# A transformer block's down projection: where a chain of weight sums is read and summed, and the order of its last joins

## The chip, the cores and the metric

The kernel runs on one core of a Trainium2 chip. A core has a matrix engine (TensorE, PE in the profile, with its weight loads shown as PEld), a vector engine (VectorE, DVE), a scalar engine (ScalarE, ACT), a general engine (GpSimd, POOL), a queue engine that mostly issues DMAs (SyncE, SP), and 16 DMA engines between the memory (HBM) and the on-chip memory (SBUF). Matmul results stand in PSUM, eight banks of 128 x 512 float32 here.

The metric is the device time of one execution in microseconds (us). Times of a kernel are given as the median of several runs; the profile is of one further execution.

## The reference

The reference is one block: a mixer (a convolution branch and a state-space branch, gated), and then a gated feed forward, each with norms and a residual. The change lies in the end of the feed forward:

```python
h = rms_norm(x, ffn_pre_g[i])
gt, up = jnp.split(h @ w_gate_up[i], 2, axis=-1)
f = (jax.nn.silu(gt) * up) @ w_down[i]
x = x + rms_norm(f, ffn_post_g[i])
```

There are 512 tokens of 1024 features; the feed forward is 2816 wide, so `w_down` has 22 strips of 128 rows, and all numbers are float32.

## The kernel before

**Products in three parts.** For float32 accuracy every operand is split in two: `hi` is a cast on ACT to the matrix engine's input type, `lo` is the remainder, which DVE computes as source minus `hi`. A product is then three matmuls (`mm3`, lines 170 to 172): hi by hi, hi by lo, lo by hi. A weight piece ("form") is therefore a read of 128 x 1024 numbers (512 KB) into a raw tile (5 buffers, tag `raw`), a cast on ACT and a subtraction on DVE.

**Feed forward.** The loop over `u` (22 units, of 84 matmuls of 256 columns) makes the gate and up projections; `second(u)` and `third(u)` are parts of a unit, and the last `third` runs after the loop. Its pieces are read by SP, in the order in which the program names them (`w_raw`, `keep_in_program_order`).

**Down projection.** The first 16 strips of `w_down` are multiplied by a scheme of seven products (p1, p5, p6, p3, p7, p2, p4 in this order) on two-by-two blocks: tokens, strips and output features each cut in halves; the blocks of the weights are s11, s12, s21, s22, each of four pieces j = 0 to 3 (512 KB each). So there are 28 jobs (p, j), each of 12 matmuls of 512 columns (2 halves of the piece by 2 token blocks by 3). The remaining six strips ("d") are multiplied directly: 8 matmul groups of 3 for each, for four token blocks t and two output halves n. Some products need sums of weight blocks:

- p1 needs s11, p5 needs s11+s12, p6 needs s11+s12+s22, p4 needs s11+s12+s22+s21. These come from a **chain**: a tile `chain[j]` is read with s11, and after each use the next block is added to it by an accumulating DMA which POOL issues (`chain_add`, line 1063).
- p3 needs s22 and p2 needs s21, read into raw tiles by SP (`raw_read`, line 1058). p7 needs s12+s22: SP reads s12 and POOL adds s22 by an accumulating DMA (line 1060).

p1 takes pieces j = 0, 1 from raw tiles (their reads and casts come before the feed forward's end, lines 1111 to 1113) and j = 2, 3 from the chain. All four chain tiles lie in the pool `pf`, which takes the room of the feed forward's operands and opens when `third` of the last unit is done (`h2.close()`, line 1115). There SP reads the chain in the order 2, 3, 0, 1 (line 1121), and s12 is added to j = 0 and 1 at once; for j = 2 and 3 the addition follows p1's form.

**Order.** Each engine runs its instructions in a fixed order. Except where the program holds an order (`keep_in_program_order` for SP's reads), a planner chooses that order at build time from the dependencies, the program order and its own estimate of durations. `prepare(n)` names the forms up to `S_AHEAD` = 4 jobs ahead and the raw reads up to `R_AHEAD` = 7 jobs ahead; a form's tiles come from nine pairs (5 `whi`, 4 `phi`). The banks x, v, y take the products as `PRODUCTS` (line 1033) lists them: p1, p6, p7 and p4 go to x, p5 and p3 to v, p2 to y; the bank z holds strips of the direct part alone. After p1, p5 and p6 ACT copies the banks into tiles `ev` (line 1158), so that they can be used again; in the trace such a tile is `evp`, a bank `sx`, `sv`, `sy`, `sz`.

**The end.** For each token block t, and first for the half n = 1, then n = 0, three last strips are multiplied; the bank is joined with its `ev` tile on DVE (line 1200). Then `scale_of` (line 1201) squares both halves on ACT (`mean_sq`, line 778), and `factor` turns the two sums into a scale `rs` (a small addition on DVE, a power on POOL, line 786). DVE multiplies both halves by the gain (line 1203), and `store(t - 1)` scales the block before, adds the residual `x2` (read from `x2d`) and sends it out (lines 1184 and 1187).

Of the kernel before, what the change touches and what calls it, by code (L numbers as in the profile page):

```python
# [10 lines left out]
F32 = mybir.dt.float32  # L11
# [3 lines left out]
ALU = mybir.AluOpType  # L15
# [3 lines left out]
P = 128  # L19
# [13 lines left out]
NF = FF // P  # L33
# [43 lines left out]
DMA_FROM = 8  # L77

NPAIR = 8
NQ = NPAIR // 2  # L80
S_AHEAD = 4
R_AHEAD = 7
# [19 lines left out]
ORDER += [("gu", _i) for _i in range(2 * EARLY_U, 2 * NF)]  # L102
ORDER += [("wd", _i) for _i in range(2 * NPAIR, NF)]
W_END = len(ORDER)
ORDER += [(_b, _j) for _b in BLOCKS for _j in range(NQ)]

# [7 lines left out]
def block_kernel(ctx: ExitStack, tc: tile.TileContext, x, xT, prm, hp, gp, w, out):  # L114
    nc = tc.nc
    act, dve, pe, pool = nc.scalar, nc.vector, nc.tensor, nc.gpsimd
# [11 lines left out]
    seq = {key: n for n, key in enumerate(ORDER)}  # L128
# [58 lines left out]
    def col(name, i):  # L187
        o = PRM_OFF[name] + i
        return prm_t[:, o : o + 1]
# [17 lines left out]
    def va_tile(name):  # L207
        return sp.tile([P, T], F32, tag="va", bufs=VA_BUFS, name=name)
# [58 lines left out]
    for k in range(NK):  # L267
# [3 lines left out]
        if k % 4 == 0:  # L271
# [3 lines left out]
            out=elo[k], in0=xk[k], scalar=col("pre_g", k), in1=ehi[k].bitcast(F32), op0=ALU.mult, op1=ALU.subtract,  # L275
# [3 lines left out]
    for k in range(NK):  # L279
# [3 lines left out]
        else:  # L283
            sq = va_tile(f"sq{k}")
# [148 lines left out]
    for j in range(NK):  # L433
# [11 lines left out]
        if j == 0:  # L445
            for k in range(NK):
                for ps, n in ((pv, "val"), (pg, "glu")):
                    wh, wl = w_get(n, 0)
                    c = slice(k * P, (k + 1) * P)
# [325 lines left out]
    def mean_sq(src, pool_, tag, n):  # L775
        ss = sm.tile([P, 1], F32, tag=f"ss{n}", bufs=2, name=f"ss{n}_{tag}")
        jk = pool_.tile([P, T], BF16, tag="jk", bufs=1, name=f"jk{n}_{tag}")
        mark["sq"] = act.activation(jk, src, AF.Square, scale=D**-0.5, accum_out=ss)
        return ss

    def factor(ss, tag):

        rs = sm.tile([P, 1], F32, tag="rs1", bufs=2, name=f"rs_{tag}")
        m = sm.tile([P, 1], F32, tag="pm1", bufs=2, name=f"pm_{tag}")
        dve.tensor_scalar(out=m, in0=ss[0], scalar1=ss[1], scalar2=RMS_EPS, op0=ALU.add, op1=ALU.add)
        pool.tensor_tensor(out=rs, in0=m, in1=neg_half[:, :1], op=ALU.pow)
        return rs

    def scale_of(srcs, pool_, tag):
        return factor([mean_sq(srcs[n], pool_, tag, n) for n in range(2)], tag)  # L790

    cols2 = [slice(0, T), slice(T, D)]
# [26 lines left out]
    def g_raw(u, i):  # L819
        n = seq[("gu", 2 * u + i)]  # L820
        for r in range(n, min(n + RAW_AHEAD, seq[("wd", 2 * NPAIR)])):
            w_raw(r)
        return raws[n]
# [17 lines left out]
    def prep_s(u):  # L841

        if u >= NF or (u, "s1") in forms:
            return
        ra, rb_ = g_raw(u, 0), g_raw(u, 1)
        (a11, a12), (a21, a22) = [(r[:, :T], r[:, T:]) for r in (ra, rb_)]
        s1_ = w2.tile([P, T], F32, tag="s1", bufs=2, name=f"s1_{u}")
        dve.tensor_tensor(out=s1_, in0=a21, in1=a22, op=ALU.add)
        dve.tensor_tensor(out=a21, in0=a11, in1=a21, op=ALU.add)
        dve.tensor_tensor(out=a11, in0=s1_, in1=a11, op=ALU.add)  # L850
        dve.tensor_tensor(out=a12, in0=a11, in1=a12, op=ALU.add)
        halve(("s2", "s4"), u, ra, pair_of_tiles())
        halve(("s1",), u, s1_, [w2.tile([P, T], F32R, tag=tg, bufs=2, name=f"{tg}_{u}") for tg in ("dhi", "dlo")])
        halve(("s3", "a22"), u, rb_, pair_of_tiles())
# [122 lines left out]

    fp = ctx.enter_context(tc.tile_pool(name="f", bufs=1, side="right"))
    f32 = fp.tile([P, NF, T], F32, name="f32")
    h2e = h2.enter_context(tc.tile_pool(name="h2e", bufs=2, side="right"))  # L980
    sg = {}
    c1, c2 = slice(0, HB), slice(HB, T)
# [21 lines left out]
    def third(u, dst):  # L1004
# [11 lines left out]
        for c, src in ((c2, dst[1][:, c2]), (c1, X[u])):  # L1016
            dve.scalar_tensor_tensor(
                out=dst[1][:, c], in0=src, scalar=-1.0, in1=g2[:, c], op0=ALU.mult, op1=ALU.mult
            )

    prev = None
    for u in range(NF):
        prep_s(u)
        prep_a(u + 1)
        prep_s(u + 1)
        if u >= EARLY_U:
            first(u)
        if prev is not None:
            third(u - 1, prev)
        prev = second(u)  # L1030
    h2_last = prev

    PRODUCTS = (("p1", "x"), ("p5", "v"), ("p6", "x"), ("p3", "v"), ("p7", "x"), ("p2", "y"), ("p4", "x"))
    jobs = [(p, j) for p, _ in PRODUCTS for j in range(NQ)] + [("d", k) for k in range(2 * NPAIR, NF)]
    w_forms, f_forms, room, chain, read = {}, {}, {}, {}, {}

    def piece_of(b, j):
        return w[seq[(b, j)]]

    def w_room(n):  # L1040
        if room:
# [9 lines left out]

    def raw_read(p, j):
        key = (p, j)
        if key in read or (p in ("p5", "p6", "p4")) or (p == "p1" and j > 1) or p == "d":
            return
        b = {"p1": "s11", "p3": "s22", "p7": "s12", "p2": "s21"}[p]
        t = read[key] = wp.tile([P, 1024], F32, tag="raw", bufs=RAW_BUFS, name=f"raw_{p}_{j}")
        tc.keep_in_program_order(nc.sync.dma_start(t, piece_of(b, j)))
        if p == "p7":
            pool.dma_start(t, piece_of("s22", j), accum_op=ALU.add)  # L1060

    def chain_add(b, j):
        pool.dma_start(chain[j], piece_of(b, j), accum_op=ALU.add)

    def w_form(n):
        p, j = jobs[n]
        if n in w_forms:
            return
        if p == "d":
            w_split(seq[("wd", j)])  # L1070
            w_forms[n] = split[seq[("wd", j)]]
            return
        raw_read(p, j)
        src = read[p, j] if (p, j) in read else chain[j]
        hi, lo = w_forms[n] = w_room(n)
        act.copy(hi, src)
        dve.tensor_tensor(out=lo, in0=src, in1=hi.bitcast(F32), op=ALU.subtract)
        follow = {"p1": "s12", "p5": "s22", "p6": "s21"}.get(p)
        if follow and (p, j) not in read:
            chain_add(follow, j)  # L1080

    def f_form(n):
        p, j = jobs[n]
# [6 lines left out]
        else:  # L1090
            hi, lo = [t.rearrange("p (k t) -> p k t", k=4) for t in f_room(n)]
            ka, kb = slice(4 * q, 4 * q + 4), slice(NPAIR + 4 * q, NPAIR + 4 * q + 4)
            a11, a12, a21, a22 = f32[:, ka, c1], f32[:, kb, c1], f32[:, ka, c2], f32[:, kb, c2]
# [22 lines left out]
    pf = ctx.enter_context(tc.tile_pool(name="pf", bufs=1))  # L1116
    room["pf"] = pf
    gpost1 = pf.tile([P, D], F32, name="gpost1")
    for j in (2, 3, 0, 1):
        chain[j] = pf.tile([P, 1024], F32, name=f"chain{j}")  # L1120
        tc.keep_in_program_order(nc.sync.dma_start(chain[j], piece_of("s11", j)))
    for j in (0, 1):
        chain_add("s12", j)
    nc.scalar.dma_start(gpost1, gp[1].partition_broadcast(P))
    room["s"] = pf.tile([P, NPAIR, HB], F32, name="s")
    ev = {(n, r): pf.tile([P, T], F32, name=f"ev{n}{r}") for n in ("p1", "p5", "p6", "mg") for r in range(2)}
# [12 lines left out]
    def prepare(n):  # L1139
        for m in range(n, min(n + S_AHEAD + 1, len(jobs))):  # L1140
            f_form(m)
            w_form(m)
        for m in range(n, min(n + R_AHEAD + 1, NQ * len(PRODUCTS))):
            raw_read(*jobs[m])

    for n, (p, j) in enumerate(jobs[: NQ * len(PRODUCTS)]):
        prepare(n)
        name = dict(PRODUCTS)[p]
        (fh, fl), (wh, wl) = f_forms[p, j // 2], w_forms[n]
        for e in range(2):  # L1150
            c, k = slice(e * T, (e + 1) * T), 2 * (j % 2) + e
            for r in range(2):
                tok = slice(r * P, (r + 1) * P)
                step(name, r, fh[:, k, tok], fl[:, k, tok], wh[:, c], wl[:, c], j == NQ - 1 and e == 1)
        if j == NQ - 1:
            for r in range(2):
# [25 lines left out]
    def store(t, mg, rs):  # L1182
        for n, c in enumerate(cols2):
            dve.scalar_tensor_tensor(
                out=x2[:, t, c], in0=mg[n], scalar=rs, in1=x2[:, t, c], op0=ALU.mult, op1=ALU.add
            )
            (nc.sync if n == 0 else nc.scalar).dma_start(out[t * P : (t + 1) * P, c], x2[:, t, c])

    for t in range(NT):
        i, r = t % 2, t // 2  # L1190
        res, mg = {}, {}
        for n in (1, 0):
            for k in range(NF - last, NF):
                d_step(t, k, n)
            b_ = banks[NAME[i, n], r]
            if (i, n) == (1, 0):
                res[n], mg[n] = b_, ev["mg", r]
            else:
                e_ = res[n] = mg[n] = ev[{(0, 0): "p1", (0, 1): "p6", (1, 1): "p5"}[i, n], r]
                dve.tensor_tensor(out=e_, in0=b_, in1=e_, op=ALU.add if (i, n) == (0, 1) else ALU.subtract)  # L1200
        rs = scale_of(res, pf, f"c{t}")
        for n, c in enumerate(cols2):
            dve.tensor_tensor(out=mg[n], in0=res[n], in1=gpost1[:, c], op=ALU.mult)
        if t:
            store(t - 1, *done)
        done = (mg, rs)
    store(NT - 1, *done)


# [77 lines left out]
```

## Time and profile before

| | us |
|---|---|
| time, median of 3 runs | 1098.06 |
| lowest and highest run | 1095.87, 1098.27 |
| time of the profiled execution | 1094.84 |
| its span, first to last instruction | 1093.1 |
| PE busy, weight loads beside it | 1058.0, 928.3 |
| DVE busy | 821.7 |
| ACT busy | 603.4 |
| POOL busy | 94.0 |

The profile is of one execution on the chip. A page shows the busy time of each engine, the span in 40 equal slices (each digit is the busy share in tenths; PEclk is the granted clock of TensorE in tenths of full speed; DMA is the busy share of the 16 DMA engines), and groups of instructions. The trace behind it can be asked for stretches, for instructions in order of time, and for what ended an engine's idle time. A row of the timeline has start and duration in us, the engine, the line of the kernel, the operation, output and inputs by the program's names (buffer numbers left out), and in brackets the engine's idle time before it and what ended that. "SPq" and "POOLq" are issues by a queue or its sequencer. Matmuls overlap: a row's duration is longer than the distance to the next.

### The profile page before, as it was taken

Reading aid. Unit: us, or ns where it says so; the run is one execution under the profiler, and the core shown is the slowest. Engines: PE = TensorE matmul, PEld = TensorE weight load, DVE = VectorE, ACT = ScalarE, POOL = GpSimd, SP = SyncE. Lnnn points to the kernel's source line nnn. Section 1 sums busy time; section 2 is a strip of 40 time slices with the busy share of each in tenths; the row PEclk is TensorE's granted clock in tenths of the full one; section 3 lists DMA queues with packets and bytes.
Section 4 is the critical chain, followed back from the end, with each engine's and each line's share of the span. In section 5 each row is a group of like instructions: output and inputs, shape, how many; then the busy total and the mean of one; then the engine's idle time right before and its main releaser. Section 6 shows DMA issues by size and latency. Waiting matters only on the chain.

```text
span 1093.1 us, 15657 instructions
## 1 busy us (share of the span) xinstructions
PE 1058.0 (97%) x6145; PEld 928.3 (85%) x6145; DVE 821.7 (75%) x1171; ACT 603.4 (55%) x968; POOL 94.0 (9%) x117
## 2 busy tenths in 40 slices
PE   8999999999999999999999999989999999969896
PEld 6888889988997899789888787879999999948785
DVE  7899995995698778788885276589987887567745
ACT  7657749686758564724323853366644544435622
POOL 2002001111111111000000000010000000012001
PEclk9999999999999999999999999999999999989998
DMA  8466653547535653451142233423332242099902
GB/s 286 130 173 195 156 132 100 155 116 198 148 98 135 163 145 97 100 152 58 54 130 87 58 116 117 153 97 116 117 126 90 97 131 82 1 274 243 292 20 77
DMA packets 39674, 142.42 MB, mean 130 GB/s; under 512 B 4656, under 2 KB 4912, under 8 KB 38576
## 3 DMA queue, kind: packets, MB, share of 16 engines
q1 hardware_dynamic: 29040, 100.46, 27.6%
q0 software_dynamic: 8352, 34.61, 15.4%
q10 hardware_dynamic: 2208, 6.36, 1.6%
q8 instruction: 48, 0.79, 0.3%
q14 instruction: 26, 0.21, 0.1%
HBM read 137.15 MB, written 4.26 MB: 129 GB/s over the span
## 4 chain that ended last, share of the span: by engine, by line
PE 75%; DVE 10%; ACT 4%; DMA 3%; issue 3%; POOL 1%; POOLq 0%; SPq 0%; DVEq 0%; ACTq 0%
PE xy L170 5%; PE xy L172 4%; PE xy L171 4%; PE pso L170 3%; PE pso L172 3%; PE pso L171 2%; PE yd L557 2%; DVE a L397 2%; PE v L170 2%; PE v L172 2%; PE v L171 2%; PE px L171 2%; PE px L172 2%; PE px L170 2%; PE pz L170 2%
## 5 line engine op out<-in xcount | busy, mean ns | idle before, releaser
L137 ACT CAST whi<-raw 128x1024 fp32r<-128x1024 f32 (+1 forms) x118 | 120.9, 1033 | 211.5 <-PE pC L171 37.9
L397 DVE SCALAR_TENSOR_TENSOR a<-v,prm_t,a 128x485 f32<-128x485 f32 (+16 forms) x240 | 180.7, 757 | 4.2 <-ACT a L394 1.4
L142 DVE TENSOR_TENSOR wlo<-raw,whi 128x1024 fp32r<-128x1024 f32 (+1 forms) x84 | 99.8, 1194 | 47.4 <-ACT whi L137 47.3
L170 PE MATMUL pz<-whi,hhi 128*128 128x256 f32 (+1 forms) x256 | 73.7, 288 | 0.8 <-DVE sg L423 0.8
L171 PE MATMUL pz<-wlo,hhi 128*128 128x256 f32 (+1 forms) x256 | 72.2, 282 | 0.0
L172 PE MATMUL pz<-whi,hlo 128*128 128x256 f32 (+1 forms) x256 | 71.9, 281 | 0.0
L828 DVE TENSOR_TENSOR wlo_g<-raw,whi_g 128x1024 fp32r<-128x1024 f32 x40 | 48.2, 1220 | 10.4 <-ACT whi_g L827 10.4
L827 ACT CAST whi_g<-raw 128x1024 fp32r<-128x1024 f32 x40 | 41.0, 1049 | 24.3 <-issue 10.5
L140 POOL DMA_DIRECT2D wlo<-in_w x34 | 30.3, 890 | 272.5 <-ACT wlo L139 169.3
L170 PE MATMUL pso<-yh,whi 128*128 128x512 f32 x128 | 50.3, 395 | 0.6 <-DVE B L474 0.6
L172 PE MATMUL px<-hhi,wlo 128*128 128x512 f32 x128 | 50.5, 394 | 0.0
L171 PE MATMUL px<-hlo,whi 128*128 128x512 f32 x128 | 50.4, 394 | 0.0
L172 PE MATMUL pso<-yh,wlo 128*128 128x512 f32 x128 | 50.2, 392 | 0.0
L170 PE MATMUL px<-hhi,whi 128*128 128x512 f32 x128 | 50.1, 391 | 0.0
L171 PE MATMUL pso<-yl,whi 128*128 128x512 f32 x128 | 50.0, 391 | 0.0
L170 PEld LDWEIGHTS pz<-whi,hhi 128*128 128x128 f32 x256 | 48.4, 189 | 1.3 <-DVE sg L423 1.0
L172 PEld LDWEIGHTS pz<-whi,hlo 128*128 128x128 f32 x256 | 48.2, 188 | 0.2
L171 PEld LDWEIGHTS pz<-wlo,hhi 128*128 128x128 f32 x256 | 48.1, 188 | 0.3
L380 ACT ACTIVATE L<-L,nacs 128x128 f32<-128x128 f32 x128 | 41.4, 392 | 6.0 <-POOL L L374 5.8
L592 DVE TENSOR_SCALAR y<-y,rs 128x256 f32<-128x256 f32 x32 | 9.4, 349 | 36.1 <-POOL rs L178 36.1
L139 ACT ACTIVATE wlo<-whi 128x1024 fp32r<-128x1024 f32 x34 | 35.9, 1056 | 0.2
L474 DVE SCALAR_TENSOR_TENSOR x<-px,prm_t,x 128x511 f32<-128x511 f32 (+2 forms) x48 | 35.4, 744 | 0.5 <-ACT x L472 0.3
(511 smaller groups left out, 3394.1 us busy)
## 6 DMA issues: line engine op xcount, KB each, us to landing
raw<-in_w SPq DMA_DIRECT2D x161, 512.0 KB, 3.7
wlo<-in_w POOLq DMA_DIRECT2D x34, 512.0 KB, 5.4
L<-scr POOLq DMA_DIRECT2D x8, 1024.0 KB, 5.3
raw_p<-in_w SPq DMA_DIRECT2D x14, 512.0 KB, 8.9
chain<-in_w POOLq DMA_DIRECT2D x12, 512.0 KB, 7.4
xT<-in_xT SPq DMA_DIRECT2D x8, 256.0 KB, 5.8
xr<-in_x ACTq DMA_DIRECT2D x4, 512.0 KB, 4.6
x2d<-xr ACTq DMA_DIRECT2D x4, 512.0 KB, 2.6
```

Source lines behind the costliest of these rows:

```text
L137: act.copy(hi[:, c], src[:, c])
L139: act.activation(lo[:, c], hi[:, c].bitcast(F32), AF.Copy, scale=-1.0)
L140: pool.dma_start(lo[:, c], w[n][:, c].bitcast(F32R), accum_op=ALU.add)
L142: dve.tensor_tensor(out=lo[:, c], in0=src[:, c], in1=hi[:, c].bitcast(F32), op=ALU.subtract)
L170: mark["pe"] = pe.matmul(ps, lh, rh, start=start, stop=False, skip_group_check=more)
L171: pe.matmul(ps, lh, rl, start=False, stop=False, skip_group_check=more)
L172: pe.matmul(ps, ll, rh, start=False, stop=stop, skip_group_check=more)
L380: act.activation(L[:, h, c, :], L[:, h, c, :], AF.Exp, bias=nacs[:, c, HG * g + h : HG * g + h + 1])
L397: return dve.scalar_tensor_tensor(out=va[j][:, d:], in0=vs[j][:, : T - d], scalar=col("dw_w", j * KC + KC - 1 - d), in1=va[j][:, d:], op0= ...
L474: dve.scalar_tensor_tensor(out=a[:, d:], in0=ps[:, : T - d], scalar=col("ssm_w", i * KS + KS - 1 - d), in1=a[:, d:], op0=ALU.mult, op1=ALU ...
L827: a_ = act.copy(hi, src)
L828: d_ = dve.tensor_tensor(out=lo, in0=src, in1=hi.bitcast(F32), op=ALU.subtract)
```

## The change

The change has three parts.

1. Three of the four chain tiles (`NCE` = 3, j = 0, 1, 2) move into a pool of their own, `ce`, which is there from the start of the feed forward's loop. Their reads of s11 are issued in the loop at unit `NF - 4`. p1 takes j = 0, 1, 2 from the chain and j = 3 from a raw tile; the fourth chain tile stays in `pf` and s12 is added to it at once. For j = 0, 1, 2 the addition of s12 follows p1's form.
2. The last sum of the chain, s21 for p4, is no longer an accumulating DMA: when p2's piece of s21 is in its raw tile and formed, DVE adds the raw tile to `chain[j]`.
3. At the end each half n is squared and multiplied by the gain right after its bank is joined, and `store(t - 1)` stands between the two halves of block t.

```diff
+NCE = 3
...
+    ce = ctx.enter_context(tc.tile_pool(name="ce", bufs=1, side="right"))
...
+    def chain_read(j, pool_):
+        chain[j] = pool_.tile([P, 1024], F32, name=f"chain{j}")
+        tc.keep_in_program_order(nc.sync.dma_start(chain[j], piece_of("s11", j)))
+
     prev = None
     for u in range(NF):
+        if u == NF - 4:
+            for j in range(NCE):
+                chain_read(j, ce)
...
-        if key in read or (p in ("p5", "p6", "p4")) or (p == "p1" and j > 1) or p == "d":
+        if key in read or (p in ("p5", "p6", "p4")) or (p == "p1" and j < NCE) or p == "d":
             return
...
-        follow = {"p1": "s12", "p5": "s22", "p6": "s21"}.get(p)
+        follow = {"p1": "s12", "p5": "s22"}.get(p)
         if follow and (p, j) not in read:
             chain_add(follow, j)
+        if p == "p2":
+            dve.tensor_tensor(out=chain[j], in0=chain[j], in1=src, op=ALU.add)
...
-    for j in (2, 3, 0, 1):
-        chain[j] = pf.tile([P, 1024], F32, name=f"chain{j}")
-        tc.keep_in_program_order(nc.sync.dma_start(chain[j], piece_of("s11", j)))
-    for j in (0, 1):
+    for j in range(NCE, NQ):
+        chain_read(j, pf)
         chain_add("s12", j)
...
-        res, mg = {}, {}
+        mg, sq = {}, {}
         for n in (1, 0):
             for k in range(NF - last, NF):
                 d_step(t, k, n)
             b_ = banks[NAME[i, n], r]
             if (i, n) == (1, 0):
-                res[n], mg[n] = b_, ev["mg", r]
+                sq[n] = mean_sq(b_, pf, f"c{t}", n)
+                mg[n] = ev["mg", r]
             else:
-                e_ = res[n] = mg[n] = ev[{(0, 0): "p1", (0, 1): "p6", (1, 1): "p5"}[i, n], r]
-                dve.tensor_tensor(out=e_, in0=b_, in1=e_, op=ALU.add if (i, n) == (0, 1) else ALU.subtract)
-        rs = scale_of(res, pf, f"c{t}")
-        for n, c in enumerate(cols2):
-            dve.tensor_tensor(out=mg[n], in0=res[n], in1=gpost1[:, c], op=ALU.mult)
-        if t:
-            store(t - 1, *done)
-        done = (mg, rs)
+                mg[n] = ev[{(0, 0): "p1", (0, 1): "p6", (1, 1): "p5"}[i, n], r]
+                dve.tensor_tensor(out=mg[n], in0=b_, in1=mg[n], op=ALU.add if (i, n) == (0, 1) else ALU.subtract)
+                sq[n] = mean_sq(mg[n], pf, f"c{t}", n)
+                b_ = mg[n]
+            dve.tensor_tensor(out=mg[n], in0=b_, in1=gpost1[:, cols2[n]], op=ALU.mult)
+            if n == 1 and t:
+                store(t - 1, *done)
+        done = (mg, factor([sq[0], sq[1]], f"c{t}"))
     store(NT - 1, *done)
```

More of the change, by code (lines that the diff above doesn't have):

```diff
@@ L1019, in third, with piece_of @@
             )
+    chain = {}
+    def piece_of(b, j):
+        return w[seq[(b, j)]]
+    def chain_read(j, pool_):
+        chain[j] = pool_.tile([P, 1024], F32, name=f"chain{j}")
+        tc.keep_in_program_order(nc.sync.dma_start(chain[j], piece_of("s11", j)))
     prev = None
     for u in range(NF):
+        if u == NF - 4:
+            for j in range(NCE):
+                chain_read(j, ce)
         prep_s(u)
@@ L1034, in block_kernel @@
     jobs = [(p, j) for p, _ in PRODUCTS for j in range(NQ)] + [("d", k) for k in range(2 * NPAIR, NF)]
-    w_forms, f_forms, room, chain, read = {}, {}, {}, {}, {}
-    def piece_of(b, j):
-        return w[seq[(b, j)]]
+    w_forms, f_forms, room, read = {}, {}, {}, {}
     def w_room(n):
```

## The prediction

> **What bounds the kernel now.** I read the page's busy tenths first, then the stretches of the span, then TensorE's gaps, then the queues that feed them.
>
> ```profile
> span 1093.1 us, 15657 instructions
> ...
> PE   8999999999999999999999999989999999969896
> ...
> PEclk9999999999999999999999999999999999989998
> DMA  8466653547535653451142233423332242099902
> ```
>
> One slice is 27.3 us. TensorE (PE) is full nearly everywhere. It drops where the DMA engines are full: slices 36 to 38, from 957 us on, the start of the down projection. The table of stretches splits that (length, then busy time of PE, PEld, DVE, ACT, POOL, then granted clock, DMA share, GB/s):
>
> ```profile
> 880.00:920.00 40.00, 40.00 (x332) 39.78 (x331) 32.39 (x50) 20.68 (x34) 0.00 (x0) 1.00 0.34 107
> 920.00:950.00 30.00, 30.00 (x251) 29.90 (x250) 19.99 (x29) 14.34 (x24) 0.00 (x0) 1.00 0.06 19
> 957.50:971.10 13.60, 11.72 (x50) 8.61 (x48) 11.37 (x11) 5.07 (x5) 2.72 (x3) 1.00 0.87 326
> 971.10:987.10 16.00, 8.30 (x26) 5.54 (x26) 6.72 (x7) 6.12 (x7) 3.47 (x4) 0.79 1.06 234
> 987.10:1014.30 27.20, 27.20 (x122) 22.53 (x121) 18.52 (x16) 14.20 (x16) 7.84 (x9) 1.00 1.05 254
> 1014.30:1030.30 16.00, 12.87 (x50) 10.15 (x49) 11.06 (x10) 12.05 (x13) 0.00 (x0) 0.89 0.96 283
> 1030.30:1052.10 21.80, 21.80 (x98) 18.07 (x97) 16.65 (x16) 10.99 (x12) 0.00 (x0) 1.00 0.35 137
> 1052.10:1084.80 32.70, 32.65 (x145) 26.70 (x143) 13.14 (x21) 6.42 (x14) 2.34 (x3) 1.00 0.09 33
> ```
>
> The last row is the direct part: 6 x 8 x 3 = 144 matmuls of 512 columns in 32.7 us, 0.227 us each. A job (one product p, one quarter j) is 12 of them, 2.72 us. From TensorE's timeline (start, duration, what; idle before and its releaser):
>
> ```profile
> 957.51 0.40 PE L170 MATMUL sx<-whi_s,whi_g 128*128 128x512 f32 x1
> ...
> 970.82 0.39 PE L172 MATMUL sx<-phi_s,fl 128*128 128x512 f32 x1
> 977.67 1.23 PE L170 MATMUL sv<-whi_s,fh 128*128 128x512 f32 x2 [6.46 <-ACT whi_s L1076]
> ...
> 987.06 0.39 PE L170 MATMUL sv<-phi_s,fh 128*128 128x512 f32 x1
> ...
> 1018.23 0.50 PE L170 MATMUL sx<-whi_s,fh 128*128 128x512 f32 x1 [3.13 <-ACT evp L1158]
> ...
> 1030.18 0.39 PE L170 MATMUL sy<-phi_s,fh 128*128 128x512 f32 x1
> ```
>
> p1 starts at 957.51, p2 (bank sy) at 1030.18: 72.7 us for 20 jobs that need 54.5. **18.2 us are lost**: p1 takes 13.5 for 10.9 (2.6 lost); p5's first two jobs, 971.05 to 987.06, take 16.0 for 5.45 (10.6 lost, the halved clock of the third row's 0.79 included); the ten jobs from p5_2 (third job of p5) to p3_3 take 27.2, nothing lost; p7's four, 1014.3 to 1030.2, take 15.9 for 10.9 (5.0 lost). After that nothing is lost up to PE's end at 1084.8. What they wait for:
>
> ```profile
> 958.22 2.31 SPq L1121 DMA_DIRECT2D chain<-in_w  x4
> 960.57 61.35 SPq L1058 DMA_DIRECT2D raw_p<-in_w  x12
> ...
> 963.39 1.04 ACT L1076 CAST phi_s<-chain 128x1024 fp32r<-128x1024 f32 x1 [2.75 <-DMA chain<-in_w]
> 966.06 1.05 ACT L1076 CAST phi_s<-chain 128x1024 fp32r<-128x1024 f32 x1 [0.66 <-DMA chain<-in_w]
> 976.58 1.04 ACT L1076 CAST whi_s<-chain 128x1024 fp32r<-128x1024 f32 x1 [9.46 <-DMA chain<-in_w]
> ...
> 1016.65 1.04 ACT L1076 CAST phi_s<-raw_p 128x1024 fp32r<-128x1024 f32 x1 [11.79 <-DMA raw_p<-in_w]
> ...
> 968.18 2.72 POOL L1063 DMA_DIRECT2D chain<-in_w  x3 [232.44 <-DMA raw_p<-in_w]
> 976.87 0.88 POOL L1063 DMA_DIRECT2D chain<-in_w  x1 [5.97 <-DMA chain<-in_w]
> ...
> 997.51 0.87 POOL L1063 DMA_DIRECT2D chain<-in_w  x1 [1.62 <-DVE plo_s L1077]
> 999.99 0.87 POOL L1063 DMA_DIRECT2D chain<-in_w  x1 [1.60 <-DVE plo_s L1077]
> 1008.38 0.86 POOL L1060 DMA_DIRECT2D raw_p<-in_w  x1 [7.53 <-DVE wlo_s L1077]
> ...
> DMA to landing us min/median/max: 7.1/7.4/12.9
> ```
>
> Tile j=2 of the chain, asked for at 958.22, is cast at 963.39: a read takes 5.2 us, the second 2.7 more. The sum s11+s12 that p5_0 needs was issued at 968.18 and is cast at 976.58. Accumulating DMAs follow each other at 997.51 and 999.99, 2.48 us apart, the loaded rate; the last row is their time from issue to landing. The last accumulate of p7 comes late because 12 chain sums stand ahead and the raw buffers come free late; ACT waits 11.79 us on it with a bank copy (L1158) behind, and TensorE waits for that.
>
> **The change, part by part.**
>
> *Early reads.* Three reads of 512 KB enter SP's queue four units before the feed forward's end (a unit is 84 matmuls; 332 take 40 us, so some 40 us before 957), ahead of its last raw pieces. They take the engines 3 x 1.3 us (worked out below) at DMA shares of 0.34 and 0.06; PE has 40.00 of 40.00 and 30.00 of 30.00 busy beside them. Cost 0; without that cover 3.9. Since p1's first two jobs were cast from raw tiles in this time already, their cost does not move. New is that s12 is added to chains 0 and 1 right after:
>
> ```profile
> 941.17 2.35 DVE L1077 TENSOR_TENSOR wlo_s<-raw_p,whi_s 128x1024 fp32r<-128x1024 f32 x2
> ```
>
> After 943.5 the DMA engines are nearly idle (0.06), so even at 12.9 us these sums land by 957. p5_0 and p5_1 then wait for nothing but their casts.
>
> *p1's tail.* Job p1_2 no longer waits for its read, but p1_3 now is cast from a raw tile that SP reads behind chain 3, whose room (pool pf) opens at 958.22 as before. It is again the second read, again there at 966.06; cast and remainder (1.05 + 1.22) end at 968.4, ten more matmuls at 970.7. I leave p1's 2.6 us where they are. Bounds: 0.3 better by that count, 1.8 worse if the gap of 2 us slows the clock as that of 3.13 did (granted 0.89 in its stretch: 0.11 x 16.0). The page "TensorE: Matmul & The Clock Gate" of the Trainium skill (Part 1: The HAM clock gate) lets the clock fall to half after an idle window of about 3.4 us; by it this gap would cost nothing, but here 3.13 was enough, so the bound stays.
>
> *p5_2 is late next.* s12 for chains 3 and 2 goes out at about 963.5 to 965, once chain 3 has landed and p1_2 is formed. The accumulates of 968.18 moved nothing while plain reads were queued:
>
> ```profile
> q1 hardware_dynamic: 224, 0.81, 102.8%
> ...
> q0 software_dynamic: 107, 0.41, 102.9%
> ```
>
> (The first row is 970 to 972, where the accumulating queue q0 has no packet; the second 976 to 978, packets, MB and share of 16 engines.) 0.81 MB in 2 us makes 1.3 us of 512 KB. Before, ten plain reads lay ahead from about 960, to 973; now seven (chain 3, p1_3, four for p3, the gains), to 969. So the two sums land near 972 and 975. If chain 2 is the second, p5_2's remainder is ready at 977.4, against 976.5 when PE wants it: 0.8 lost. Bounds: 0 (chain 2 first) and 4.9 (the 12.9 us of the last row behind 965). The page "DMA: Bandwidth & Descriptors" of the Trainium skill (Anatomy of one DMA — SWDGE path) fits 2.0 us plus bytes at 436 GB/s: by that a sum would land 3.2 us after issue, an estimate, the 0.8 would go, and the forecast would be 0.8 lower. This trace has 7.1 at least.
>
> *p5, p6, p3.* The s22 sums run at 2.48 against 2.72 a job; s22_0 lands near 977.5, its remainder is ready at 980 and wanted at 982.7. Margins of 1 to 3 us; I count 0. So 10.6 becomes 0.8: **gain 9.8**.
>
> *s21 on VectorE.* Four accumulates (4 x 2.48 us of all DMA engines) leave POOL's queue and become four additions 128x1024:
>
> ```profile
> L1098 DVE TENSOR_TENSOR f<-f x2: 1218/1219/1220, 960.5 to 970.6; 128x1024 f32<-128x1024 f32 x2
> ```
>
> 4 x 1.22 = 4.9 us. DVE is free for 5.1 of the 21.8 us in which p2 and p4 run and for 19.6 of the next 32.7, and no job p4 is cast before p2. Cost 0; if DVE is behind, up to 4.9 before p4. The raw tiles of p2 are held 1.2 us longer; behind them stand x2d and six pieces for the direct part, needed 20 us later.
>
> *p7.* Its four accumulates now follow six sums instead of ten: p7_0's lands by 990. p7_1 waits for p3_0's raw buffer (free about 992.5 after p6_3's cast), a read of 5.2 and an accumulate of 7.1: there at 1004.8, remainder at 1007.1, wanted at 1007.2 (971.05 + 0.8 + 13 x 2.72); p7_2 and p7_3 follow at 2.48 against 2.72. So the 5.0 go: **gain 5.0** (bounds 0 and 5.0).
>
> *The end.* Each half is now squared, multiplied and, for token block t, followed by the store of t-1 as soon as its bank is joined.
>
> ```profile
> 1084.84 0.60 ACT L778 ACTIVATE jk_c<-sx 128x512 bf16<-128x512 f32 x1 [1.49 <-PE sx L172]
> 1085.56 0.63 ACT L778 ACTIVATE jk_c<-evp 128x512 bf16<-128x512 f32 x1
> ...
> 1085.08 1.41 DVE L1184 SCALAR_TENSOR_TENSOR f<-evp,rs_c,f 128x512 f32<-128x512 f32 x2 [0.44 <-POOL rs_c L786]
> 1086.41 0.68 DVE L1203 TENSOR_TENSOR evmg<-sx,gpost 128x512 f32<-128x512 f32 x1
> ...
> 1087.36 0.86 POOL L786 TENSOR_TENSOR rs_c<-pm_c,neg_half 128x1 f32<-128x1 f32 x1 [2.31 <-DVE pm_c L785]
> 1088.25 0.75 DVE L1184 SCALAR_TENSOR_TENSOR f<-evmg,rs_c,f 128x512 f32<-128x512 f32 x1 [0.44 <-POOL rs_c L786]
> ```
>
> Now POOL's power for the last factor starts at 1087.36, after the other half's square and both multiplications behind a store; the two last halves end at 1088.25 + 1.4 = 1089.7. With that square ahead of PE's end, the shortest chain is 1084.84 + 0.8 (square) + 0.2 + 0.1 + 0.86 + 1.4 (two halves) = 1088.3 instead of 1089.7: 1.4 gained at most. The store of t=2 (1.41) and the last multiplication still share DVE there, so I take 0.8; lower bound -0.7, one multiplication more ahead of the factor.
>
> **Sum:** 9.8 + 5.0 + 0 + 0.8 = 15.6 us. The profiled execution took 1094.84 us (span 1093.1 and 1.7 around it): 1079.2. The median shown is 1098.06, 3.2 above it, so in its terms **1082.4 us**.
>
> **Rivals.**
>
> *Less: the sums still late* (5 to 12 us gained, 1086 to 1093). The tiles j=2 and 3 and p7_1 keep part of the old waits: with the bounds of p5_2 (4.9) and of p7 (5.0) the gain is 15.6 - 4.1 - 5.0 = 6.5, 1091.6. For it: margins of 0.2 to 3 us, ACT in order (a cast that waits on a DMA holds those behind it). Against: six accumulates leave the crowded stretch.
>
> *More* (1076 to 1080): p1's 2.6 go too and the end gives 1.4: 18.8, 1079.3; with the lowest of the runs shown, 1095.87, 1077.
>
> *It doesn't do what it says* (within 1093 to 1096): if the planner's order lets the first sums wait until the room pf opens, only the four s21 sums go; p7's 5.0 at most are gained, 1093. Against: tiles and POOL are free at 943.
>
> *Slower: accumulates one at a time.* With fewer candidates at once, POOL could issue each only after the last has landed, at 7.4 us and not 2.48. Ten of them (six sums, four for p7) from 963.5 end at 1037.5, p7_3 would start 2.3 later, 1039.8, where now it starts at 1027.5: 12.3 slower, 0.8 back at the end, 1109.6. It decides from 6.2 us each ((1027.5 - 2.3 - 963.5) / 10). For it: every chain is read, summed, cast and summed again. Against: 2.48 between issues, and four chains in turn.
>
> **How the numbers follow.** Forecast (1080 to 1086) 0.63; less 0.15; more 0.09; not as said 0.07; slower 0.06. A measurement of this kernel tells about 0.2% (2.2 us) from no change. "Not as said" and "less" reach into that band with 0.04. So faster 0.90, same 0.04, slower 0.06. The range takes the forecast with its bounds, most of "less" and half of "more": 1077 to 1091.
>
> **What would show it.** Right: no PE gap of 6 us near 971 and none of 3 us before p7; POOL's first sums near 942, eight (not twelve) issues of L1063's kind from chains, four DVE additions beside p2; p2 starting near 1015; squares of the first half ahead of PE's end. Wrong: an ACT cast of a chain tile that waits over 3 us after 971, a POOL queue whose issues stand 7 us apart, p1's gap grown beyond 3 us with a granted clock under 0.9, or an end later than 5 us after PE's last matmul.

## The result and the profile after

| | before | after |
|---|---|---|
| median, us (runs) | 1097.97 (4) | 1088.34 (4) |
| lowest and highest run | 1095.87, 1098.27 | 1087.39, 1089.29 |
| profiled execution | 1094.84 | 1087.39 |
| p1's start to p2's start (20 jobs, 54.4 without waits) | 72.7 | 64.8 |
| p1's start to the direct part's start | 94.4 | 86.6 |
| end of PE to end of DVE | 4.9 | 5.2 |

The change is faster by 0.8%: ratio 0.9916, 95% interval 0.9899 to 0.9934. That is 9.6 us by the medians, against 15.6 forecast. The profiled executions differ by 7.5, and their stages by the same: 1089.66 - 957.51 = 132.15 us from p1's start to DVE's end before, 1082.60 - 958.06 = 124.54 after. p1's start varies from trace to trace, 957.5 to 961.0 in all but two kernels of this study (962.1 and 962.6 in those named "p1 from raw"), so below stages are compared, not times from the span's start.

The page of the kernel after, its span and busy tenths:

```profile
span 1085.6 us, 15651 instructions
...
PE   8999999999999999999999999999999999989996
...
PEclk9999999999999999999999999999999999989999
DMA  7466643647535653452133222423333342167912
```

Slice 36 reads 8 where it read 6, and slice 38 is full. TensorE's timeline of the kernel after has these waits, and the first matmuls of p1, p2 (bank sy) and the direct part:

```profile
958.06 0.40 PE L171 MATMUL sx<-whi_s,whi_g 128*128 128x512 f32 x1
...
972.18 0.79 PE L171 MATMUL sx<-phi_s,fh 128*128 128x512 f32 x1 [4.44 <-ACT phi_s L1087]
973.44 0.79 PE L172 MATMUL sx<-plo_s,fh 128*128 128x512 f32 x1 [0.47 <-DVE plo_s L1088]
...
977.87 0.63 PE L173 MATMUL sx<-phi_s,fl 128*128 128x512 f32 x1
...
995.97 0.50 PE L173 MATMUL sx<-whi_s,fl 128*128 128x512 f32 x1 [0.78 <-DVE fl L1120]
...
1022.85 0.39 PE L171 MATMUL sy<-phi_s,fh 128*128 128x512 f32 x1
...
1044.63 0.39 PE L171 MATMUL sy<-whi,fh 128*128 128x512 f32 x1
```

Before p7 nothing is left of the 5.0 us. p5_0 and p5_1 don't wait for their sums. But p1_3 waits 4.44 + 0.47 us, longer than anything in p1 before, and then runs at a slowed clock: its rows stand 0.43 us apart, not 0.227. In p1_2, p1_3, p5_0 and p5_1 together (part of p5_0 the planner put ahead of p1_3) 8.5 us are lost, nearly all at p1_3, where p1 lost 2.6; p5_2 to p6_2 lose 1.8 more. So 10.3 of the 18.2 us remain. ACT's timeline of the kernel after has the casts behind these losses; the first row is p1_3's raw piece, the last is p5_2's sum:

```profile
971.08 1.04 ACT L1087 CAST phi_s<-raw_p 128x1024 fp32r<-128x1024 f32 x1 [7.14 <-DMA raw_p<-in_w]
977.35 2.00 ACT L1087 CAST whi_s<-chain 128x1024 fp32r<-128x1024 f32 x2 [5.23 <-DMA chain<-in_w]
981.09 1.05 ACT L1087 CAST phi_s<-chain 128x1024 fp32r<-128x1024 f32 x1 [1.74 <-DMA chain<-in_w]
```

SP asks for p1_3's raw piece at 960.02 as second read, as foretold, but it is there at 971.08, not 966. POOL's timeline of the kernel after shows what is new in that time:

```profile
943.34 0.94 POOL L1074 DMA_DIRECT2D chain<-in_w  x1 [206.57 <-DVE wlo_s L1088]
944.48 0.86 POOL L1074 DMA_DIRECT2D chain<-in_w  x1 [0.20 <-issue]
959.51 0.86 POOL L1074 DMA_DIRECT2D chain<-in_w  x1 [14.17 <-DVE f L1019]
960.98 0.88 POOL L1074 DMA_DIRECT2D chain<-in_w  x1 [0.61 <-DVE wlo_s L1088]
968.00 0.87 POOL L1074 DMA_DIRECT2D chain<-in_w  x1 [6.14 <-PE sx L172]
969.97 0.86 POOL L1074 DMA_DIRECT2D chain<-in_w  x1 [1.10 <-issue]
```

The rows of 959.51 and 960.98 are s22 for j = 0 and 1. Since the first two chains have their s12 early, p5_0 and p5_1 are cast in the feed forward's last unit too, and the planner's order lets their next sums go out at once, wanted only for p6, some 20 us later. They stand ahead of s12 for j = 3 and 2 (968.00 and 969.97), wanted first. The DMA queues in three stretches of the kernel after (packets, MB, share of the 16 engines' time; q0 carries the accumulates, q1 SP's reads, q10 the read of the gains that ACT issues), 963 to 964, 964 to 965, and 967 to 969:

```profile
q1 hardware_dynamic: 32, 0.13, 45.0%
q10 hardware_dynamic: 33, 0.14, 38.5%
...
q0 software_dynamic: 11, 0.05, 25.8%
...
q0 software_dynamic: 80, 0.27, 67.8%
q1 hardware_dynamic: 78, 0.26, 35.3%
```

In the first stretch q0 has no packet; in the second the sum of 959.51 begins to move, 5 us after its issue (its first packets stand between 964.5 and 964.75). From then on the plain reads get a third of the engines. Until 965 the gains' read (512 KB, issued at 959.53) moves beside chain 3's read and p1_3's too, though the gains are first used at 1064.7.

The end of the kernel after, from the timeline of DVE and POOL:

```profile
1080.26 0.20 DVE L786 TENSOR_SCALAR pm_c<-ss_c,ss_c 128x1 f32<-128x1 f32 x1
1080.61 0.54 POOL L787 TENSOR_TENSOR rs_c<-pm_c,neg_half 128x1 f32<-128x1 f32 x1 [2.92 <-DVE pm_c L786]
1081.18 0.75 DVE L1195 SCALAR_TENSOR_TENSOR f<-evmg,rs_c,f 128x512 f32<-128x512 f32 x1 [0.72 <-POOL rs_c L787]
1081.85 0.75 DVE L1195 SCALAR_TENSOR_TENSOR f<-evp,rs_c,f 128x512 f32<-128x512 f32 x1
```

PE ends at 1077.43; the power starts 3.2 us later, where it started 2.6 after PE's end before (1087.36 - 1084.75). A store and both multiplications now stand on DVE ahead of the small addition (1080.26).

### The profile page after: what moved, and what is told of

Same layout as the page of the kernel before. It is cut to its first block, busy times and chain, and to the rows that moved or that the text cites. A ratio compares the mean times of both kernels' runs of the same rounds, so it can differ in the third digit from the quotient of the medians.

```text
span 1085.6 us, 15651 instructions
## 1 busy us (share of the span) xinstructions
PE 1057.1 (97%) x6145; PEld 927.7 (85%) x6145; DVE 826.5 (76%) x1175; ACT 603.3 (56%) x968; POOL 89.0 (8%) x113
## 4 chain that ended last, share of the span: by engine, by line
PE 74%; DVE 12%; DMA 4%; ACT 3%; issue 2%; POOL 1%; POOLq 0%; DVEq 0%; ACTq 0%; SPq 0%
PE xy L171 4%; PE xy L172 3%; PE xy L173 3%; PE pso L171 3%; PE pso L173 3%; PE pso L172 3%; PE yd L558 2%; DMA chain<-in_w 2%; PE px L172 2%; PE px L173 2%; PE pz L171 2%; PE px L171 2%; PE pz L172 2%; PE pz L173 2%; DMA raw<-in_w 2%
## 5 line engine op out<-in xcount | busy, mean ns | idle before, releaser
L829 DVE TENSOR_TENSOR wlo_g<-raw,whi_g 128x1024 fp32r<-128x1024 f32 x40 | 48.2, 1220 | 10.1 <-ACT whi_g L828 10.0
```

The lines of the kernel that those rows point to most:

```text
L829: d_ = dve.tensor_tensor(out=lo, in0=src, in1=hi.bitcast(F32), op=ALU.subtract)
```

## The experiments

A table first: losses are TensorE's time over 2.72 us a job, from the start of p1 to that of p2, put to the wait's place. "Tail" is PE's end to DVE's end.

| kernel | median (range), us | ratio to before, 95% | p1 to p2 | p1 to direct | tail | main losses |
|---|---|---|---|---|---|---|
| before | 1097.97 (1095.87-1098.27) | | 72.7 | 94.4 | 4.9 | p1 to p5_1 13.2, p7 5.0 |
| after | 1088.34 (1087.39-1089.29) | 0.9916 [0.9899, 0.9934] | 64.8 | 86.6 | 5.2 | p1_3 8.5, p5_2 to p6_2 1.8 |
| raw read early | 1093.73 (1092.22-1096.72) | 0.9975 [0.9964, 0.9987] | 67.1 | 90.4 | 5.2 | p5_2 10.1, p4_0 1.4 |
| sums as written | 1088.14 (1086.56-1091.16) | 0.9933 [0.9907, 0.9959] | 63.4 | 85.7 | 5.2 | p1_3 2.6, p5_2 6.1 |
| s21 only | 1093.81 (1092.45-1096.36) | 0.9978 [0.9966, 0.9989] | 68.3 | 91.9 | 4.9 | p1 to p5_1 13.5, p7 0.4, p4_0 1.8 |
| old tail | 1088.42 (1086.66-1090.12) | 0.9926 [0.9907, 0.9946] | 65.3 | 87.1 | 4.9 | as after |
| p3 reads behind | 1088.68 (1088.54-1090.53) | 0.9932 [0.9913, 0.9951] | 64.8 | 87.0 | 5.2 | as after |
| p1 from raw | 1089.50 (1087.24-1091.86) | 0.9934 [0.9913, 0.9955] | 62.7 | 85.9 | 5.4 | p5_2 to p6_0 7.2 |
| the same, power first | 1090.63 (1088.78-1091.44) | 0.9942 [0.9924, 0.9959] | 63.9 | 85.6 | 4.3 | p5_2 to p6_0 7.7 |
| s12 first | 1087.62 (1086.66-1088.15) | 0.9917 [0.9903, 0.9930] | 64.1 | 85.9 | 5.2 | p1_3 2.7, p5_3 to p6_1 7.0 |
| s12 first, raw early | 1090.14 (1088.08-1090.53) | 0.9937 [0.9923, 0.9950] | 62.4 | 86.9 | 5.2 | p5_2 to p6_2 6.9, p4_0 2.6 |
| the same, power first | 1088.88 (1088.03-1090.10) | 0.9927 [0.9914, 0.9941] | 62.7 | 88.8 | 4.3 | p5_2 to p6_2 7.1, p4_0 to p4_1 4.3 |
| half sums | 1085.34 (1083.79-1086.97) | 0.9894 [0.9878, 0.9910] | 61.9 | 83.7 | 5.2 | p1_3 7.5 |
| p1_2 early, power first | 1087.54 (1085.54-1090.69) | 0.9918 [0.9901, 0.9935] | 64.5 | 87.2 | 4.0 | p1_3 7.2, p6_1 to p7_3 2.7 |

**Raw read early.** p1_3's raw piece is read ahead of the feed forward's last `third`:

```diff
+    for j in range(NCE, NQ):
+        raw_read("p1", j)
     f_form(0)
```

> The read of p1's fourth piece is put ahead of chain 3's read on SP, into the feed forward's end, so that it shares the DMA engines with nothing. Theory A (the changed kernel issues the s22 sums of j = 0 and 1 already at 959.5 and 961.0, and these and everything else behind 959 share the DMA engines, so one late transfer is followed by the next): TensorE's wait of 4.4 us for that piece goes, but the sum s11+s12 of j = 2, which lands near 981 in the changed kernel, is late next, and p2 starts only 1 to 2 us earlier: about 1087. Theory B (that one read is all that is late): p2 starts some 7 us earlier, about 1081.

The wait at p1_3 went, and by the medians the kernel was 5 us slower than the change. TensorE's timeline and then ACT's, in the kernel with the raw read early:

```profile
985.16 0.80 PE L171 MATMUL sv<-phi_s,fh 128*128 128x512 f32 x1 [6.51 <-ACT phi_s L1087]
```

```profile
980.27 1.99 ACT L1087 CAST whi_s<-chain 128x1024 fp32r<-128x1024 f32 x2 [12.53 <-DMA chain<-in_w]
```

The same 6.5 us stand at p5_2, whose sum now comes last. In the change the wait at p1_3 had hidden these late sums behind it.

**Sums as written.** `chain_add` is put under `keep_in_program_order`, so that POOL issues s12 for j = 3 and 2 ahead of s22.

> Only POOL's order is held: the s12 sums of j = 3 and 2 go out before the s22 sums of j = 0 and 1, which now are issued at 959.5 and 961.0. Theory A (these two sums slow the reads behind which p1's fourth piece stands): that piece lands near 967.5 in place of 971, TensorE's gap in p1 falls from 4.9 us to under 2, the sum for p5_2 comes near 976, and the s22 sums of j = 0 and 1 are late next; 3 to 5 us faster than the changed kernel, about 1084. Rival (the piece is late because its read now waits for the room behind the feed forward): it still lands near 971, no gain, 1088.

p1_3 now loses 2.6, the very value of the prediction, and 6.1 appear at p5_2, the slowed clock after its wait included. The median is that of the change (1088.14 to 1088.34).

**s21 only.** The kernel before with part 2 of the change alone.

> The kernel before with the second part alone (s21 added on VectorE). If four accumulates fewer on POOL free p7 of its wait, the 5.0 us lost in p7 go: 1093. Rival (p7 waits for raw buffers that come free late, not for POOL): the wait before p7_0's fourth matmul stays at 3 us, 1098.

The 4.5 us lost in p7_0 (its wait of 3.13 us and the slowed clock behind it) fell to 0.4: p7's term stands by itself. But 1.8 us are lost ahead of p4_0, which the whole change doesn't lose.

**Old tail.** The change with the end as before.

> The changed kernel with the end (joins, squares, gains, stores) as before. By the prediction's term the new end is worth 0.8 us, so this takes 0.8 longer than the changed kernel, 1089.1. Theory now, from the two traces (from PE's end to DVE's end 4.9 us before, 5.2 after): the new end is worth nothing; within 0.4 us of the changed kernel, and the last power on POOL starts about 2.6 us after PE's end here and 3.2 in the changed kernel.

POOL's timeline of the kernel with the old tail, last power:

```profile
1081.21 0.86 POOL L787 TENSOR_TENSOR rs_c<-pm_c,neg_half 128x1 f32<-128x1 f32 x1 [2.31 <-DVE pm_c L786]
```

PE ends at 1078.63 there, so the power is 2.6 behind it and DVE's end 4.89: the new end is 0.28 us longer than the old, and the median can't tell the two apart (1088.42, 1088.34).

**p3 reads behind.** p3's four plain reads are issued by POOL, so that fewer reads stand behind p1_3's in SP's queue.

> p3's four reads, which SP issues from 960.5 on though p3 needs them only near 1000, are issued by POOL, in its order among and behind the sums. Theory A (what is late is the sum of all transfers between 959 and p5_3's form: in the changed kernel nine plain reads and seven accumulates share the engines up to 981): with three or four reads less ahead, p1's fourth piece lands near 968 in place of 971 and the sum for p5_2 near 976 in place of 981; from p1's start to p2's start about 60 us, where the changed kernel takes 64.8 and the one before 72.7; about 1084. Rival (a sum takes as long as it takes once issued, whatever lies beside it): 64 to 65 us, 1088.

ACT's timeline of that kernel:

```profile
971.19 1.04 ACT L1090 CAST phi_s<-raw_p 128x1024 fp32r<-128x1024 f32 x1 [6.77 <-DMA raw_p<-in_w]
```

The piece was no earlier. What stands behind it in the queue doesn't delay it. The sums of j = 0 and 1 still moved beside it (issued at 959.99 and 961.46); what they cost is shown by "s12 first" below.

**p1 from raw**, and **the same, power first**. All four pieces of p1 are read into raw tiles, s12 goes to the chains 0 to 2 before p1 (the four reads and the three sums stand ahead of `f_form(0)`); in the second the small addition of the factor stands ahead of both multiplications.

> All four pieces of p1 are cast from raw tiles that SP reads in the feed forward's end, and s12 is added to chains 0 to 2 there too, so that of the seven transfers that p1 and p5 wait for only chain 3 and its s12 are left behind 959. It reads 1.5 MB more. Theory A: no wait in p1 and before p5_0 to p5_2, one of at most 3 us before p5_3 (chain 3 lands near 967, its sum near 977 where PE wants it at 977); p1's start to p2's start 55 to 58 us, 1080 to 1082. Rival (the casts and remainders on ACT and DVE, or the s22 sums, are late next by as much): 62 us or more, 1086.

> The kernel of the run before with one thing more: at the end the small addition that feeds POOL's power stands ahead of the two multiplications by the gain. In the changed kernel it stands behind them and behind the store of t=2, and from PE's end to DVE's end are 5.2 us. If that order is what took the prediction's 0.8 us, the same distance is 4.4 us here, and the time 0.8 less than that kernel's. Rival (the stores, multiplications and the join are all due on DVE there, and their sum is the bound in any order): 5.0 to 5.2.

p1 loses only 1.1, but ACT waits 11.94 us for the chain of j = 3 with p6's casts queued behind it, and 7.2 us are lost from p5_2 to p6_0. Besides, a unit of the feed forward (902.12 to 915.04) took 12.9 us, not 10.2. DVE's timeline of that kernel, and q0 from 905 to 910:

```profile
910.43 0.69 DVE L849 TENSOR_TENSOR s<-raw 128x512 f32<-128x512 f32 x1 [4.09 <-DMA raw<-in_w]
...
q0 software_dynamic: 222, 0.78, 78.4%
```

The three early sums, issued from 899.3 on, take the engines there, and a piece of the feed forward's own weights is late. p1's raw pieces are no part of this: they are asked for from 919.9 on.

The power first makes the tail 1.1 us shorter; the median, 1090.63 to 1089.50, shows nothing of it.

**Three orders more.** In "s12 first" the sums are held in order and s12 for j = 3 is named with p1_3's form, so that all s12 stand ahead of all s22. "Raw early" adds the early read of the first experiment, "power first" the end of the one above.

```diff
         follow = {"p1": "s12", "p5": "s22"}.get(p)
-        if follow and (p, j) not in read:
+        if follow:
             chain_add(follow, j)
...
     for j in range(NCE, NQ):
         chain_read(j, pf)
-        chain_add("s12", j)
```

> The change with its accumulates in another order: s12 of jobs 0 to 3 all ahead of s22 of jobs 0 and 1, held in the order written. Theory (plain reads and accumulates share the engines, accumulates take about two thirds of their time, so what counts is which accumulate goes first): the job p1_3 still waits some 2 us for its raw piece, the wait at p5_2 is smaller than the 2.7 us of the run with the order s12_0, s12_1, s22_0, s22_1 held; first phase to second 61 to 63 us, down projection (from p1's start) 84 to 85.5, median 1086 to 1087.5. Rival (the waits only move from job to job, since the accumulates together take a fixed time): first to second phase 63 to 65, median 1087 to 1089.

> As the run above, and p1_3's raw read issued ahead of chain 3's first read. Theory: no wait at p1_3; its s12 is issued by 966 and has landed by 976, p5_2 and p5_3 nearly without wait, at most 1 to 3 us left at p6_0; first to second phase 57 to 60 us, median about 1082 to 1084. Rival (the waits move): p1_3's wait goes and comes back at p5_2 to p6_0, as when the raw read alone was early (67.1 from first to second phase), at best 62 to 65, median 1087 to 1089.

> As the run above, and in the end the factor's small addition ahead of both multiplications. Theory: the time of the run above less about 0.8 us (end of TensorE to end of VectorE 4.3 us in place of 5.2). Rival: the end of VectorE comes earlier, but the stores' landing doesn't, and the median is that of the run above within 0.3 us.

ACT's timeline and then TensorE's, in the kernel with s12 first:

```profile
967.57 1.04 ACT L1087 CAST phi_s<-raw_p 128x1024 fp32r<-128x1024 f32 x1 [3.64 <-DMA raw_p<-in_w]
```

```profile
968.67 0.50 PE L171 MATMUL sx<-phi_s,fh 128*128 128x512 f32 x1 [0.95 <-ACT phi_s L1087]
969.93 0.51 PE L172 MATMUL sx<-plo_s,fh 128*128 128x512 f32 x1 [0.76 <-DVE plo_s L1088]
980.41 0.50 PE L172 MATMUL sv<-wlo_s,fh 128*128 128x512 f32 x1 [0.23 <-DVE wlo_s L1088]
985.99 0.80 PE L171 MATMUL sx<-phi_s,fh 128*128 128x512 f32 x1 [2.78 <-ACT fh L1118]
```

No sum moves beside p1_3's read now, and it is cast 7.6 us after its issue at 960.0, not 11.1. But p5_3 to p6_1 lose 7.0 us, and p1 to p2 is 64.1, 0.7 less than with the change: of the expectations the rival's came true, 63 to 65. With the raw read early as well p1 loses 1.1 and p5_2 to p6_2 6.9, and one wait more appears. TensorE's timeline of that kernel, and its stretch from 1024 (length, then PE, PEld, DVE, ACT, POOL, clock, DMA share, GB/s):

```profile
1036.43 0.47 PE L171 MATMUL sx<-phi_s,fh 128*128 128x512 f32 x1 [2.46 <-DVE evp L1172]
```

```profile
1024.00:1045.00 21.00, 18.54 (x82) 15.05 (x82) 21.00 (x21) 12.39 (x13) 0.00 (x0) 1.00 0.52 179
```

DVE is busy 21.00 of 21.00 us, and p4's bank is joined late because of it (the bank x is held by `evp`'s join, line 1172). The power first took 0.85 us from the tail here too (4.30 to 5.15); the ranges of the two kernels' runs overlap, and its trace lost 1.9 us more ahead of the direct part.

**Half sums** and **p1_2 early.** The first is the change with each chain sum cut to its first 512 columns (the other half of each sum is left out, so only its time is of use):

```diff
-        pool.dma_start(chain[j], piece_of(b, j), accum_op=ALU.add)
+        pool.dma_start(chain[j][:, 0:512], piece_of(b, j)[:, 0:512], accum_op=ALU.add)
```

The second is "s12 first" with the split tiles of p1_2 and p1_3 swapped against those of p5_0 and p5_1, and the power first:

```diff
-            pool_, tags, bufs = ((wp, ("whi", "wlo"), W_BUFS), (room["pf"], ("phi", "plo"), 4))[n % 9 in (2, 3, 6, 8)]
+            pool_, tags, bufs = ((wp, ("whi", "wlo"), W_BUFS), (room["pf"], ("phi", "plo"), 4))[n % 9 in (4, 5, 6, 8)]
```

> The change with every chain sum cut to half its bytes (columns 0 to 511 of 1024; the other half of the sums is left out). Theory (between 964 and 988 us the DMA engines are full, and the accumulates' share of them is what the casts wait for): each sum takes the engines some 1.2 us and not 2.5, p1_3's raw piece is cast by 969 and not at 971.1, TensorE loses 2 to 5 us from the first phase to the second and not 10.3, so p1 to p2 57 to 60 us, median 1081 to 1084. Rival (what counts is the path of one sum, from its issue by POOL over a fixed time to its landing, the cast and the next sum, whatever its size): p1 to p2 63 to 65 us as with whole sums, median 1087 to 1089.

> As the run with s12 of jobs 0 to 3 ahead of all s22, and in addition jobs p1_2 and p1_3 take their split tiles from the pool that is open in the feed forward (p5_0 and p5_1 take theirs from pf), so that p1_2's form and its s12 come in the feed forward's last unit; the end has the factor's small addition ahead of both multiplications. Theory (the engines' time between 964 and 988 is the bound, so a sum that starts at 960 and not at 965.5 is out of it): the waits at p5_3 and p6_0 (6.6 us together) shrink to 1 to 3, p1_3 keeps 2 to 4; p1 to p2 58.5 to 61.5 us, to the direct part 80 to 83; end of TensorE to end of VectorE 4.3; median 1082 to 1085. Rival (the waits only move): p1_3 waits 5 to 7 us beside the early sum, p1 to p2 63 to 65, median 1086 to 1088.

TensorE's timeline with half sums, and two rows of its queues from 967 to 969:

```profile
973.08 0.50 PE L171 MATMUL sx<-phi_s,fh 128*128 128x512 f32 x1 [2.87 <-ACT phi_s L1087]
974.34 0.80 PE L172 MATMUL sx<-plo_s,fh 128*128 128x512 f32 x1 [0.76 <-DVE plo_s L1088]
```

```profile
q1 hardware_dynamic: 108, 0.38, 50.6%
q0 software_dynamic: 90, 0.18, 50.5%
```

The time fell between the two expectations: p1 to p2 61.9, the theory said at most 60, the rival at least 63. What it lost is all at p1_3 and its slowed clock; from p5_2 on nothing is lost, where the change loses 1.8 though it lost 1.0 more at p1_3. So the loss of p5_2 to p6_2 shrinks with the sums' bytes; p1_3's piece still shares with two sums. With p1_2 early one whole sum, issued at 959.1, moves beside p1_3's read. TensorE's timeline of that kernel:

```profile
970.80 1.22 PE L171 MATMUL sx<-whi_s,fh 128*128 128x512 f32 x2 [4.70 <-ACT whi_s L1087]
```

p1_3 loses 7.2, p6_1 and what follows 2.7, and p1 to p2 is 64.5: the rival's 63 to 65 again.

**Together.** The read of p1_3's piece, from issue to cast, took 7.6 us with no sum beside it, 9.5 with two half sums, 10.1 with one whole, 11.1 with two. And in the five kernels that, up to the direct part, differ from the change only in the order of reads, sums and casts (raw early, as written, s12 first, the same with raw early, p1_2 early) p1 to p2 takes 62.4 to 67.1 us, p1 to the direct part 85.7 to 90.4: the change's 64.8 and 86.6 lie among them. The stretch from 964 to 988 (length, the engines, clock, DMA share), first in the change, then with s12 first, then with half sums:

```profile
964.00:988.00 24.00, 18.82 (x68) 14.02 (x67) 12.80 (x12) 8.48 (x10) 4.32 (x5) 0.86 1.03 270
```

```profile
964.00:988.00 24.00, 18.94 (x74) 13.69 (x73) 14.67 (x13) 8.77 (x10) 6.09 (x7) 0.95 1.05 274
```

```profile
964.00:988.00 24.00, 20.25 (x74) 15.67 (x73) 15.25 (x15) 12.07 (x14) 4.69 (x6) 0.86 0.93 246
```

All five orders keep the DMA engines full for these 24 us (shares 1.00 to 1.05), as the change (1.03) and the kernel before (1.05) do; half sums leave some room (0.93). No kernel that computes the whole was measurably faster than the change: the lowest medians, 1087.54 and 1087.62, lie within its runs' range.

## Why the prediction was right, and where it wasn't

The direction held, and the median lies in the range, in its upper part: 1088.34 where 1082.4 was forecast. What came is the rival *less: the sums still late*, by a way that it doesn't name; the range holds the result because it took in most of that rival, not because the sum was right. Three of the prediction's own signs of being wrong showed: a cast of a chain tile waited 5.23 us (977.35), p1's gap grew to 4.44 us with a granted clock of 0.86 from 964 to 988, and DVE ended 5.2 us after PE.

**p7: right.** Gain 5.0 of 5.0; by part 2 alone the loss in p7_0 fell from 4.5 to 0.4.

**Early reads: right in cost, not in effect.** p1's start moved by 0.55 us, less than it varies between runs. But what the early reads set free was followed only up to s12. The next link was not: p5_0 and p5_1, ready, are formed at once, and their s22 is issued at 959.5 and 961.0.

**p1's tail and p5_2: the step that failed.** The prediction said that p1_3's piece "is again the second read, again there at 966.06", and that accumulates "moved nothing while plain reads were queued". The second was read off a stretch in which q0 had no packet (970 to 972), where the sum of 968.18 stood behind a run of plain reads. As a rule it fails: in the change sums and reads share the engines from 964.5 to 980. Nor does a sum begin a fixed time after its issue: with idle engines its first packet came about 1.5 us later (943.34 to 944.75 in the change), beside queued reads 3.7 to 5 us later (966.92 to 970.5 in "sums as written", 959.51 to 964.5 in the change). In the kernel before and in "s12 first", where the sums were issued behind the reads, they began as these ran out (972.3 and 969.8); what sets the lag stays open. What counts here: the two sums that the prediction put to 977 went out at 959.5 and 961.0, about when p1_3's read did (960.02), and stood beside it. p1 to p5_1 lost 8.5 where 2.6 + 0 were counted, p5_2 to p6_2 1.8 where 0.8 was: 6.9 us. Of p1_3's loss 2.9 are the slowed clock after the gap of 4.44 (978.29 - 972.18 = 6.1 us for 2.72 of matmuls and a wait of 0.47).

Had the sums gone out in the order that the prediction took for granted, p1 would have lost 2.7, as it said; "s12 first" shows that. But p5_3 to p6_1 then lose 7.0, not 0.8 and 0. That margins of 1 to 3 us were counted as 0 on a queue whose engines are full was the second half of the error: the work was summed job by job by its latest wait, and never as DMA time that must pass between 958 and p6. One bound was mis-added, too: 965 + 12.9 + 1.05 + 1.22 is 980.2, against the 976.5 at which PE wants p5_2, so p5_2 could lose 3.7 by it, not 4.9, and *less* comes to 1090.4, not 1091.6.

**s21 on VectorE: right here, with no cover to spare.** The change loses nothing ahead of p4. Its stretch beside p2 and p4:

```profile
1024.00:1045.00 21.00, 21.00 (x94) 17.39 (x93) 21.00 (x20) 11.76 (x13) 0.00 (x0) 1.00 0.46 165
```

DVE is full there. Five variants (raw early, s21 only, p1 from raw, s12 first with raw early and its power first) lost 1.3 to 4.3 us ahead of p4 or in it.

**The end: wrong sign.** 0.8 gained was forecast, 0.3 was lost, within the stated bound of -0.7. The chain of 1.4 us less needs the small addition ahead of the multiplications. With it there the tail was 0.85 to 1.1 us shorter, but the medians of the two pairs moved by 1.3 down and 1.1 up, so no gain is shown.

**The sum:** 15.6 - 6.9 - 1.1 = 7.6 us, the difference of the stages (132.15 - 124.54). The medians differ by 9.6; that the profiled execution of before lay 3.1 under its median and that of after 1.0 makes the other 2 us, which no stage shows. In the four later sets of runs the kernel before had medians of 1095.85 to 1097.33 (7 to 19 runs each), so 1097.97, of four runs, lies high.

What stays open: which share of the remaining 10.3 us is the engines' time and which the chain's path (read, cast, sum, cast). Half sums took away 2.9 of it, and the combination of half the bytes with s12 first was not tried. Nor was the gains' read issued later: it takes 5.5% of the engines from 958 to 988, which is 1.65 us of all 16, and moves beside chain 3's read and p1_3's. The kernel before has the same read there, so it doesn't explain the change.

## What to carry to other kernels

Where transfers are moved earlier, follow what they set free one link further: the work that becomes ready early issues transfers of its own, and these share the engines with the one that is wanted first. Add up the transfer time of a crowded stretch as one sum against its length, before the waits are counted one by one. Here, with the engines full, five other orders moved the wait; none ended measurably earlier, and one ended 5 us later. And a queue that moves nothing in a stretch may not have begun yet; look at its issue before taking it for a rule of who goes first.

## What the runs showed of the hardware

Accumulating DMAs and plain reads share the DMA engines by packets, not by time: 80 packets of q0 and 78 of q1 from 967 to 969 in the change, at 67.8% and 35.3% of the engines' time, since a packet of a sum takes them about twice as long (0.678 x 32 / 80 = 0.27 us of one engine against 0.353 x 32 / 78 = 0.14). The Trainium skill's page "DMA: Bandwidth & Descriptors" (Queues, rings and completion order) says that each engine goes round between the queue rows that have work, a packet at a time; these counts agree with it.

A sum of half the bytes takes a little more than half the time. The queue of the sums while four of them move beside plain reads, first in the change from 964 to 981, then with half sums from 967 to 980:

```profile
q0 software_dynamic: 576, 2.10, 62.0%
```

```profile
q0 software_dynamic: 576, 1.05, 43.8%
```

That is 0.620 x 17 / 4 = 2.6 us of all 16 engines for a whole sum and 0.438 x 13 / 4 = 1.4 us for a half one. The number of packets is the same, at half the size each, so cutting the bytes in half saved 46% of a sum's time.
